# First shift and scale in two halves, small loads on SyncE's queue, branch hints for the first expert and inside overflow blocks

## The chip, the cores and the metric

The kernel runs on one core of a Trainium2 chip. The metric is the device time of one execution in microseconds (us); three executions were timed before the change, and one more was profiled. Engines are named as in the profile: PE is the matrix engine (PEld its weight loads), DVE the vector engine, ACT the scalar engine, POOL the GpSimd engine, SP the engine that issues most transfers. A "q" behind an engine's name means its sequencer (branches, semaphores, issues), not its datapath.

## What is computed

A sequence of 256 tokens with 1024 channels goes through a first block of two layers and a second block of one layer, all in float32. Cut to what matters here:

```python
def first_block(x, c, ...):
    for layer in range(2):
        mod = silu(c) @ w_ada[layer] + b_ada[layer]            # 1024 -> 6 * 1024
        sh1, sc1, g1, sh2, sc2, g2 = split(mod, 6)
        hcur = rms_norm(x, norm1_g) * (1 + sc1) + sh1
        mix = ...   # layer 0: dilated attention and gated MLP; layer 1: convolution and stick-breaking attention
        x = x + g1 * mix
        hcur = rms_norm(x, norm2_g) * (1 + sc2) + sh2
        x = x + g2 * hierarchical_moe(hcur, ...)                # 16 experts, 2 per token, routed by small matrices
    return rms_norm(x, final_norm_g)
# second_block: one layer with eight projections, a recurrence, window attention, and a final norm
```

Every weight is used once, so some 350 MB are streamed from memory in one execution.

## The kernel before

**Streams.** The large weights are cut into tiles of 1 MB (128 x 2048 float32) and loaded by SP through a ring of buffers, in one fixed list (`plan`) that is also the order of their use. `load` (L208) issues the next tile as soon as a buffer is free. All of SP's transfers share one queue, q1, in the order of their issue. POOL's transfers are on another queue, q0. `bcast` (L335) loads a row into all partitions.

**Shift and scale.** `ada` (a generator, matmuls on L351) multiplies the conditioning vector with w_ada: eight tiles of 256 columns give sh1 and sc1 of a layer, 16 records of the profile for each tile (8 matmuls). Behind the eighth, ACT copies the sum (`e`, L364), PE turns it into columns (L369), and `done` (L391 to L393, DVE) makes the vectors b1 and a1 of 8 columns each, one column for 128 channels. In layer 0 this stands at the very start. The rest of w_ada follows as filler work between other matmuls, by a generator (`fill_with`, `some_fill`).

**First projection.** `to_hT` (L536) transposes the scaled x on PE (L553); for each of eight groups k of 128 channels ACT makes `xh` = a1 * x + b1, rounded (L556), DVE the same unrounded (`hf`, L560) and the difference `xl` (L546). The projections (`proj_ws`, L461 to L463, output `pw`; `half_ts`, L478 to L480, output `pt`) multiply xh and xl with weights that ACT and DVE split likewise into `wh` (L444) and `wl` (L447).

**Before the experts.** The last projection of a layer is `out_proj` (`pt` again); its epilogue on DVE is L570 and L571. `moe_consts` loads the router's matrix `wr` (L600) and multiplies it by the shift b2 on PE (`rbias`, L603); `logits` transposes the new x (`tr`, L615) and multiplies it with `wr`.

**Experts.** `moe` runs the 16 experts in order on batches of 64 slots. An expert's hidden half is made by `half` (L806, L807 on PE, L818 on DVE), turned by `turn` (L825 on PE, L826 on DVE), and multiplied down and scattered. Ahead of each expert's second half stands an If (L907, `more`) on the number of its overflow blocks: a block of 64 more slots runs in it, and a further If stands inside that one. Engines read the count from memory (`values_load`, L939 and L968). For experts 1 to 15 a hint that names the coming branch and its direction is given on PE at L969, right behind the load of the count. The first expert's branch and the inner ones have none. Before the first expert's branch DVE and ACT copy x into the accumulators `z` (L949, L951).

The order of instructions on PE, ACT and DVE is set by a list scheduler when the kernel is built, but for stretches under `manual_schedule`, which keep the order of the code.

## Time and profile before

| | |
|---|---|
| median of three runs | 1229.49 us (1227.82, 1229.49, 1229.55) |
| profiled execution | 1227.14 us, of which 1225.4 us span |
| mean granted clock of PE | 0.977 of full speed |
| PE busy | 1118.5 us, 91% |
| DVE, ACT busy | 52%, 34% |
| moved by DMA | 353 MB, 288 GB/s in the mean |

The span is the time from the first to the last instruction of the profiled execution; its own time is 1.7 us longer. [...]

### The profile page before, as it was taken

What the parts mean: (1) busy time and instruction counts of PE and PEld (TensorE: products, weight loads), DVE (VectorE), ACT (ScalarE), POOL (GpSimd) and SP (SyncE); (2) the same over time, 40 slices, a digit from 0 to 9 for tenths busy, and PEclk for the clock granted to TensorE, in tenths of its full rate; (3) what the DMA queues carried; (4) which work ended last, traced back from release to release, by engine and by line L of the source; (5) the groups of instructions that cost most, each with busy time, mean ns of one, the idle gap of its engine ahead of it and who ended that gap; (6) DMA issues with size and microseconds to landing.
All of it is one profiled execution on the core that took longest, in us unless ns stands there. A gap on an engine that the chain in (4) does not pass through costs nothing. (4 is left out here: it accounts for less than half of the span.)

```text
span 1225.4 us, 20762 instructions
## 1 busy us (share of the span) xinstructions
PE 1118.5 (91%) x8164; PEld 798.3 (65%) x8168; DVE 643.1 (52%) x1485; ACT 415.4 (34%) x801; POOL 16.6 (1%) x37
## 2 busy tenths in 40 slices
PE   4899998898999889999987999898889999999996
PEld 2687575454555458867654555554478889887895
DVE  2665463232332258977622333232398787656666
ACT  1433532111111144365311211111356535445553
POOL 1000000000000000000000000000000000000000
PEclk9899998999999999999998999999999989999999
DMA  9999688999999986768855999998455435544340
GB/s 346 419 421 362 248 333 329 405 381 391 399 416 418 383 315 252 264 210 313 345 219 214 404 403 416 390 400 311 163 208 181 143 128 179 182 144 165 127 172 35
DMA packets 50184, 353.38 MB, mean 288 GB/s; under 512 B 5776, under 2 KB 5952, under 8 KB 8416
## 3 DMA queue, kind: packets, MB, share of 16 engines
q1 hardware_dynamic: 47952, 344.14, 72.0%
q0 software_dynamic: 1776, 6.48, 1.7%
q8 instruction: 105, 1.72, 0.6%
q14 instruction: 63, 0.52, 0.1%
q10 hardware_dynamic: 288, 0.52, 0.1%
HBM read 350.07 MB, written 1.05 MB: 287 GB/s over the span
## 5 line engine op out<-in xcount | busy, mean ns | idle before, releaser
L807 PE MATMUL gu<-ring,xg 128*64 128x256 f32 x1024 | 246.2, 395 | 6.3 <-issue 6.3
L806 PE MATMUL gu<-ring,xg 128*64 128x256 f32 x1024 | 246.2, 395 | 1.4 <-issue 1.3
L461 PE MATMUL pw<-xh,wh 128*128 128x256 f32 x736 | 213.1, 291 | 9.6 <-ACT wh L444 4.3
L463 PE MATMUL pw<-xh,wl 128*128 128x256 f32 x736 | 211.4, 288 | 1.7 <-DVE wl L447 1.7
L462 PE MATMUL pw<-xl,wh 128*128 128x256 f32 x736 | 210.6, 287 | 0.0
L447 DVE TENSOR_TENSOR wl<-ring,wh 128x1024 fp32r<-128x1024 f32 x144 | 175.3, 1222 | 66.2 <-ACT wh L444 62.3
L806 PEld LDWEIGHTS gu<-ring,xg 128*64 128x64 f32 x1024 | 141.8, 142 | 73.7 <-issue 16.3
L444 ACT ACTIVATE wh<-ring 128x1024 fp32r<-128x1024 f32 x114 | 120.0, 1058 | 144.4 <-PE pw L462 83.8
L807 PEld LDWEIGHTS gu<-ring,xg 128*64 128x64 f32 x1024 | 142.3, 142 | 22.3 <-issue 12.7
L461 PEld LDWEIGHTS pw<-xh,wh 128*128 128x128 f32 x736 | 142.6, 194 | 21.4 <-issue 11.3
L463 PEld LDWEIGHTS pw<-xh,wl 128*128 128x128 f32 x736 | 143.0, 194 | 6.0 <-DVE wl L447 3.5
L462 PEld LDWEIGHTS pw<-xl,wh 128*128 128x128 f32 x736 | 142.9, 194 | 1.8 <-DVE xl L546 1.0
L832 PE MATMUL y<-ring,ht 128*64 128x512 f32 (+1 forms) x576 | 128.7, 564 | 7.0 <-DVE ht L826 5.0
L818 DVE SCALAR_TENSOR_TENSOR hd<-hs,gc,gu 64x256 f32<-64x256 f32 x64 | 30.7, 479 | 176.5 <-ACT hs L817 176.5
L817 ACT ACTIVATE hs<-gu 64x256 f32<-64x256 f32 x66 | 24.9, 378 | 270.4 <-PE gu L807 270.4
L351 PE MATMUL ada<-ring,zc 128*32 128x256 f32 x960 | 70.8, 400 | 19.8 <-DVE rt L518 13.7
L832 PEld LDWEIGHTS y<-ring,ht 128*64 128x64 f32 x576 | 40.4, 137 | 53.2 <-issue 33.4
L842 ACT ACTIVATE Y<-yf 64x512 fp32r<-64x512 f32 (+1 forms) x72 | 42.7, 593 | 91.3 <-DVE yf L839 90.4
L478 PE MATMUL pt<-wh,xh 128*128 128x512 f32 x144 | 57.9, 403 | 0.6 <-ACT wh L444 0.4
L843 DVE TENSOR_TENSOR Y<-yf,Y 64x512 fp32r<-64x512 f32 (+1 forms) x72 | 46.2, 641 | 22.7 <-ACT Y L842 21.3
L826 DVE COPY ht<-hidT 128x128 f32<-128x128 f32 x66 | 19.2, 292 | 73.2 <-PE hidT L825 73.2
L351 PEld LDWEIGHTS ada<-ring,zc 128*32 128x32 f32 x960 | 27.9, 112 | 45.6 <-DVE sp__111 L326 13.7
(392 smaller groups left out, 1579.8 us busy)
## 6 DMA issues: line engine op xcount, KB each, us to landing
ring<-moe SPq DMA_DIRECT2D x192, 1024.0 KB, 9.1
ring<-ada SPq DMA_DIRECT2D x60, 1024.0 KB, 7.8
ring<-b_z SPq DMA_DIRECT2D x24, 1024.0 KB, 4.8
ring<-b_x SPq DMA_DIRECT2D x12, 1024.0 KB, 4.8
ring<-od_q SPq DMA_DIRECT2D x8, 1024.0 KB, 7.9
ring<-ev_q SPq DMA_DIRECT2D x6, 1024.0 KB, 19.8
ring<-ev_v SPq DMA_DIRECT2D x4, 1024.0 KB, 17.0
ring<-ev_o SPq DMA_DIRECT2D x4, 1024.0 KB, 10.5
```

The source lines that it names most:

```text
L351: T.matmul(p[32 * j:32 * j + 32, :256], zc[:, k, 7 - r:39 - r], w[:, k], start=start and k < 4, stop=stop and k >= 4, skip_group_check=True)
L444: S.activation(h, w, AF.Copy)
L447: V.tensor_tensor(l, w, h.bitcast(F32), op=OP.subtract)
L461: T.matmul(p, hk, xh[:, k], start=k == 0, stop=False)
L462: T.matmul(p, hk, xl[:, k], start=False, stop=False)
L463: T.matmul(p, lk, xh[:, k], start=False, stop=k == KD - 1)
L478: T.matmul(p[t], xh[:, k, n], hk, start=k == 0, stop=False)
L806: T.matmul(p[gs_], xg[:, k], wg[:, k], start=k == 0, stop=k == KD - 1)
L807: T.matmul(p[us], xg[:, k], wu[:, k], start=k == 0, stop=k == KD - 1)
L832: T.matmul(y[64 * h:64 * h + 64, cs], ht[:, k], wd[:, k % 2, h, cs], start=k == 0 and cs.start == 0, stop=k == 3, skip_group_check=cs != s ...
L842: S.activation(Y[a, h, cs], yf[a, cs], AF.Copy)
L843: V.tensor_tensor(Y[b, h, cs], yf[a, cs], Y[a, h, cs].bitcast(F32), op=OP.subtract)
```

## The change

It has three parts. The first one: the eight tiles of layer 0's first shift and scale are loaded in the order 0, 1, 4, 5, 2, 3, 6, 7, and a1 and b1 of layer 0 become two tiles of four columns each, so that the first four tiles give the first half of both. The second: `rbias` (20 KB), `g2dup` (two times 128 KB) and `wr` of both layers (80 KB each) are loaded by SP and no longer by POOL. The third: hints on PE for the first expert's branch and inside overflow blocks.

```diff
@@ -120,7 +120,7 @@
-    A["ada0"] = _ada(i["w_ada"][0])
+    A["ada0"] = _ada(i["w_ada"][0], (0, 1, 4, 5, 2, 3, 6, 7))
@@ -354,22 +354,23 @@
-        if cols:
+        for n, done in cols:
             p = bank(fill["tag"][0], "ada")
-            for t in range(8):
-                ada_rows(p, tile_of(t), t, t == 0, t == 7)
-                if t == 7:
+            for t in range(n):
+                ada_rows(p, tile_of(t), t, t == 0, t == n - 1)
+                if t == n - 1:
                     e = adap.tile([P, 256], F32, name="e", tag="e")
                     S.activation(e, p[:, :256], AF.Copy)
...
             for c in range(2):
-                T.matmul(p[:, 256 + 8 * c:264 + 8 * c], e[:, c * P:c * P + P], sel8, start=True, stop=True, skip_group_check=True)
-            cols(p[:, 256:272].rearrange("p (c t) -> p t c", c=2))
+                T.matmul(p[:, 256 + n * c:256 + n + n * c], e[:, c * P:c * P + P], sel8[:, 0:n], start=True, stop=True, skip_group_check=True)
+            done(p[:, 256:256 + 2 * n].rearrange("p (c t) -> p t c", c=2))
             yield
-            t0 += 8
+            t0 += n
@@ -387,11 +388,18 @@
+        if isinstance(a, tuple):
+            return [part(a[h], b[h], 4 * h) for h in range(2)]
+        return [part(a, b, 0)]
@@ -428,7 +436,9 @@
+    for n in ("a1_0", "b1_0"):
+        mod[n] = tuple(cst.tile([P, 4], F32, name=f"{n}_{h}") for h in range(2))
@@ -553,11 +564,11 @@
-            high = S.activation(xh[:, k], q, AF.Identity, scale=a[:, k:k + 1], bias=b[:, k:k + 1])
+            high = S.activation(xh[:, k], q, AF.Identity, scale=at(a, k), bias=at(b, k))
@@ -588,8 +599,6 @@
-    bcast(rbias.rearrange("p a b -> p (a b)"), A["rows"][0, 0:40])
@@ -597,7 +606,7 @@
-        G.dma_start(wr, A[f"rt{l}"])
+        nc.sync.dma_start(wr, A[f"rt{l}"])
@@ -859,7 +868,9 @@
-            def more_tokens(e, w, b):
+            def more_tokens(e, w, b, nv):
+                if b < 3:
+                    tc.mark_branch_hint_location(f"more{l}_{e}_{b + 1}", hint=nv > b, engines=[mybir.EngineType.PE])
@@ -904,9 +915,9 @@
-                    with tc.If(nv > b - 1, label=None if b > 1 else f"more{l}_{e}"):
+                    with tc.If(nv > b - 1, label=f"more{l}_{e}" + (f"_{b}" if b > 1 else "")):
@@ -937,6 +948,7 @@
             nv = nc.values_load(xi[0:1, 0:1], min_val=0, max_val=3)
+            tc.mark_branch_hint_location(f"more{l}_0", hint=nv > 0, engines=[mybir.EngineType.PE])
@@ -1040,13 +1052,14 @@
+        bcast(rbias.rearrange("p a b -> p (a b)"), A["rows"][0, 0:40], nc.sync)
...
-            bcast(g2dup[64 * h:64 * h + 64], A["drows"][5, h * 512:h * 512 + 512])
+            bcast(g2dup[64 * h:64 * h + 64], A["drows"][5, h * 512:h * 512 + 512], nc.sync)
```

Since the scheduler orders the instructions, the change shows in two places. On ACT, at the first shift and scale, this stood before (`e` is the copy of the projected sum, `wh` the rounded part of the first projection's weights):

```order
L364 ACTIVATE e<-ada 128x256
L556 ACTIVATE xh<-tr,b_0_175,a_0_174 128x256 x5
L444 ACTIVATE wh<-ring 128x1024
L556 ACTIVATE xh<-tr,b_0_175,a_0_174 128x256
L444 ACTIVATE wh<-ring 128x1024
L556 ACTIVATE xh<-tr,b_0_175,a_0_174 128x256 x2
L444 ACTIVATE wh<-ring 128x1024
```

After the change there are two copies `e`, the first four `xh` stand ahead of the second, and two `xh` stand between it and the first `wh`:

```order
L365 ACTIVATE e<-ada 128x256
L567 ACTIVATE xh<-tr,b_0_0_176,a_0_0_174 128x256 x4
L365 ACTIVATE e<-ada 128x256
L567 ACTIVATE xh<-tr,b_0_1_177,a_0_1_175 128x256 x2
L454 ACTIVATE wh<-ring 128x1024
L567 ACTIVATE xh<-tr,b_0_1_177,a_0_1_175 128x256
L454 ACTIVATE wh<-ring 128x1024
L567 ACTIVATE xh<-tr,b_0_1_177,a_0_1_175 128x256
```

Ahead of the first `wh` of ACT there were five `xh` behind the last `e`; there are two now. On PE, at the end of layer 0's attention and the start of its output projection (`ptt` and `po` are the attention's transposes and outputs, `pt` the output projection, `ada` the next layer's shift and scale), this stood before:

```order
L409 MATMUL ada<-e,sel_107 64x256
L603 MATMUL rbias<-wr,b_0_177 128x20 x3
L1154 MATMUL po<-pb,vg 64x256
L1155 MATMUL po<-pb,vg 64x128
L603 MATMUL rbias<-wr,b_0_177 128x20 x5
L1151 MATMUL ptt<-ident,sb 128x128 x3
L478 MATMUL pt_1414<-wh,xh 128x512
L479 MATMUL pt_1414<-wh,xl 128x512
L480 MATMUL pt_1414<-wl,xh 128x512
L1154 MATMUL po<-pb,vg 64x256
L1155 MATMUL po<-pb,vg 64x128
L478 MATMUL pt_1415<-wh,xh 128x512
L1151 MATMUL ptt<-ident,sb 128x128 x3
```

And this stands there after the change:

```order
L417 MATMUL ada<-e,sel_107 64x256
L1167 MATMUL po<-pb,vg 64x256
L1168 MATMUL po<-pb,vg 64x128
L1164 MATMUL ptt<-ident,sb 128x128 x3
L1167 MATMUL po<-pb,vg 64x256
L1168 MATMUL po<-pb,vg 64x128
L1164 MATMUL ptt<-ident,sb 128x128 x3
L1167 MATMUL po<-pb,vg 64x256
L1168 MATMUL po<-pb,vg 64x128
L351 MATMUL ada<-ring,zc 32x256 x16
L612 MATMUL rbias<-wr,b_0_179 128x20 x8
L488 MATMUL pt_1424<-wh,xh 128x512
```

The eight `rbias` matmuls and the first `pt` stood among the attention's last steps. Now they follow the last `po`, behind 16 `ada` matmuls that stood later: one of them among the second half's `pt`, 15 behind the last of these. On SP, `rbias` now follows `rows`, the two `g2dup` stand behind eight further tiles, and `wr` of layer 0 stands between the last `ada` tile and the first of the experts' tiles.

## Rows read from the trace of the kernel before

**Rows 1.** Windows over the front of layer 0, columns in the first row.
```profile
core 0: us, PE busy (x) PEld busy (x) DVE busy (x) ACT busy (x) POOL busy (x), PEclk, DMA share, GB/s
2.00:14.00 12.00, 0.27 (x4) 0.23 (x8) 5.53 (x43) 3.43 (x12) 2.29 (x5) 1.00 0.98 300
14.00:26.00 12.00, 11.62 (x112) 6.85 (x104) 1.91 (x15) 0.00 (x0) 0.00 (x0) 1.00 1.02 421
...
44.00:130.00 86.00, 85.23 (x666) 65.74 (x658) 53.17 (x123) 33.49 (x57) 0.63 (x1) 1.00 0.96 387
```

**Rows 2.** PE's timeline: start, length, engine, line, tiles, records, idle time before and releaser.
```profile
32.05 1.52 PE L351 MATMUL ada<-ring,zc 128*32 128x256 f32 x16 [0.58 <-DMA ring<-ada]
...
38.67 0.58 PE L461 MATMUL pw<-xh,wh 128*128 128x256 f32 x1 [3.97 <-ACT wh L444]
```

**Rows 3.** ACT's timeline of the same stretch.
```profile
35.29 2.38 ACT L556 ACTIVATE xh<-tr,b,a 128x256 fp32r<-128x256 f32 x5 [1.25 <-DVE a L393]
37.55 1.07 ACT L444 ACTIVATE wh<-ring 128x1024 fp32r<-128x1024 f32 x1
```

**Rows 4.** POOL's queue, 0 to 70 us: packets, MB, share of 16 engines.
```profile
q0 software_dynamic: 176, 0.36, 3.4%
```

**Rows 5.** PE's timeline around the router's bias product.
```profile
140.52 1.29 PE L603 MATMUL rbias<-wr,b 128*128 128x20 f32 x10
...
143.16 0.77 PE L478 MATMUL pt<-wh,xh 128*128 128x512 f32 x1
...
147.91 0.38 PE L1155 MATMUL po<-pb,vg 128*64 128x128 f32 x2
```

**Rows 6.** PE's timeline behind the last product of the output projection.
```profile
172.14 1.93 PE L351 MATMUL ada<-ring,zc 128*32 128x256 f32 x30
...
174.56 0.99 PE L615 MATMUL tr<-ident,x 128*128 128x128 f32 x7 [0.24 <-DVE x L571]
```

**Rows 7.** The experts' Ifs (L907), sequencers: count, shortest/median/longest ns, first and last start.
```profile
L907 PEldq COMPARE_BRANCH  x34: 80/444/5846, 194.5 to 868.4; - x34
```

**Rows 8.** The same line, layer 1's first expert alone.
```profile
L907 PEldq COMPARE_BRANCH  x1: 5583/5583/5583, 610.5 to 610.5; - x1
...
L907 DVEq EVENT_SEMAPHORE  x1: 21/21/21, 614.5 to 614.5; - x1
L907 PEldq EVENT_SEMAPHORE  x1: 51/51/51, 616.1 to 616.1; - x1
```

**Rows 9.** PE's timeline: its first work behind five Ifs.
```profile
200.65 0.44 PE L825 MATMUL hidT<-ident,hd 64*128 64x64 f32 x2 [3.71 <-PEq L907]
...
232.70 0.30 PE L825 MATMUL hidT<-ident,hd 64*128 64x64 f32 x2 [2.15 <-PEq L907]
...
283.32 0.31 PE L825 MATMUL hidT<-ident,hd 64*128 64x64 f32 x2 [1.81 <-PEq L907]
...
359.04 0.31 PE L825 MATMUL hidT<-ident,hd 64*128 64x64 f32 x2 [0.47 <-DVEq L907]
...
654.74 0.45 PE L825 MATMUL hidT<-ident,hd 64*128 64x64 f32 x2 [3.57 <-PEq L907]
```

**Rows 10.** Windows behind these Ifs and layer 1's first, columns as in the first.
```profile
200.00:210.00 10.00, 9.11 (x46) 4.61 (x46) 1.25 (x4) 0.38 (x1) 0.00 (x0) 0.66 0.68 234
230.00:240.00 10.00, 7.54 (x45) 4.01 (x45) 1.67 (x4) 0.38 (x1) 0.00 (x0) 0.83 1.00 402
280.00:290.00 10.00, 7.88 (x56) 4.24 (x53) 1.91 (x5) 0.75 (x2) 0.00 (x0) 1.00 0.97 375
610.00:620.00 10.00, 5.93 (x37) 3.33 (x36) 3.61 (x11) 1.58 (x4) 0.00 (x0) 0.84 0.64 243
650.00:660.00 10.00, 6.05 (x28) 3.45 (x30) 1.36 (x4) 0.15 (x1) 0.00 (x0) 0.71 0.49 175
```

**Rows 11.** Issues of 134 to 160 us: line, count, KB each, median us to landing.
```profile
ring<-ada SPq DMA_DIRECT2D x1, 1024.0 KB, 4.8
```

## The prediction

> **What bounds the kernel now.** The page's share of busy time (91% for PE, in the table above) says that PE is the engine to follow, but not where it waits, so I read three kinds of views: the timeline and windows of the start, since all the rest waits for the first shift and scale; PE's timeline where the change moves instructions; and the Ifs of the experts, on the sequencers and on PE's timeline behind them.

> At the start the DMA is the limit. From 2 to 14 us its engines are fully taken (share 0.98), yet they move 300 GB/s, against 421 GB/s from 14 to 26 us at the same share [rows 1]. PE waits for the last projection tile until 32.05 us, and then idles 3.97 us before the first product at 38.67 us, released by ACT's `wh` [rows 2]. ACT makes five `xh` in 2.38 us ahead of that `wh` [rows 3]. From 44 to 130 us PE is busy for 85.23 of 86.00 us [rows 1]: from there it is PE, not a tile, that sets the pace, and a head start at 38 us is carried along.

> In the expert stage the long waits of PE stand behind Ifs. PE's branch instruction takes 444 ns in the median and 5846 ns at most [rows 7]. The unhinted branch of layer 1's first expert takes 5583 ns [rows 8]. PE's first work behind the unhinted ones came after 3.71 us (layer 0's first expert) and 3.57 us (an inner If, behind the only overflow block that ran); a hinted one shows 0.47 us [rows 9].

> **The change part by part. First, the small loads.** At the full rate the bytes of 2 to 14 us would have taken 12 x (421 - 300) / 421 = 3.4 us less [rows 1]. POOL's queue moved only 0.36 MB, but took 3.4% of the engines over 70 us, which is 2.4 us of all of them [rows 4]. If these loads stand behind, the eight tiles land earlier by something between 0.36 MB / 421 GB/s = 0.9 us (the bytes alone) and 3.4 us (the whole deficit). I take 2.9, the middle between the 2.4 us that the queue held the engines and the whole deficit, since other short rows (`cols`, x) run in that time too. In their new places these loads can cost later tiles up to the same 2.4 us. That is hidden as long as PE is the bound, and between 44 and 130 us PE's idle time was 0.8 us in all.

> **The two halves.** Three `xh` fewer stand between the last `e` and the first `wh`. One costs (37.55 - 35.29) / 5 = 0.45 us [rows 3], so `wh` comes 1.4 us sooner; the other `xh` run while tiles 5 to 8 land. The additional `e`, two matmuls and three small DVE operations lie in the same wait. If the wait before the first product then ends on DVE's `hf` or `wl`, this is 0. Together the start gains 4.3 us (bounds 0.9 and 4.8).

> **What the scheduler moved at the output projection.** Before, PE began `pt` at 143.16 us among the attention's last steps, and seven `pt` had run when the last `po` ended at 148.29 us [rows 5]. A `pt` takes (172.14 - 148.29) / 89 = 0.27 us, other matmuls included, so the projection stood as if started at 146.4 us without a hole [rows 5, 6]. Now PE first finishes the attention, then runs 16 `ada` and eight `rbias` matmuls, then `pt`. Sixteen `ada` are 32 records, at 1.93 us for 30 [rows 6] 2.1 us; eight `rbias` are 16 records, at 1.29 us for ten [rows 5] again 2.1 us. The attention's end moves up from 148.3 to 146.4 us, since the seven `pt` are gone from between, so `pt` begins at 146.4 + 4.2 = 150.6 us: a loss of 4.2 us. It is 2.9 if the ten records of `rbias` that stood ahead of the last two transposes had also delayed the chain, and 6.1 if the chain, which waits for DVE, doesn't move up at all. I take 4.2. Before, 30 of these `ada` records filled PE's wait for the new x on DVE, from 172.14 us to the transposes at 174.56 us [rows 6]; that wait stays and is empty now. Behind pauses of this size the clock sometimes fell: after 1.81 us of waiting it was 1.00 over the next window, after 2.15 us it was 0.83, or 1.7 us of 10 lost [rows 9, 10]. I put the mean, 0.85 us, on it (bounds 0 and 1.7). So the front of layer 0 as a whole: 4.3 - 4.2 - 0.85 = -0.75 us, a slight loss.

> **The hints.** With a quick branch, PE still has to wait for DVE, which passes the end of the same If only behind its copies into `z`. In layer 1 DVE is through at 614.5 us and PE at 616.1 us [rows 8]: 1.6 us can be gained, and about 2.0 us of pause stay. Layer 0's pause is 0.1 us longer (3.71 us, [rows 9]; the copies are the same), so 1.7 there. The inner If has no such copies: 3.57 - 0.47 = 3.1 us [rows 9]. Together 6.4 us (bounds 0 and 6.4). The hint instruction itself is one of a sequencer that runs ahead of PE here; I give it nothing. The same wait for DVE is what comes next in both first experts.

> Behind these pauses PE ran at a lower clock: 0.66, 0.84 and 0.71 of full speed in the windows from 200, 610 and 650 us [rows 10], so that up to 3.4 + 1.6 + 2.9 = 7.9 us of the 30 were lost. The inner If's pause goes nearly wholly. The two others shrink to about 2.0 us, after which by the two rows above 0 to 1.7 us are still lost, 1.7 for both in the mean: 6.2 us would come back. I take two thirds, 4.2 us, because part of that low clock stems from PE's other pauses there, as at 200 to 210 us before work picks up (bounds 0 and 7.9).

> **Sum.** -0.75 + 6.4 + 4.2 = 9.85 us. The profiled execution would take 1227.14 - 9.85 = 1217.3 us. It lay 2.35 us under the median of the runs shown, so the median goes to 1229.49 - 9.85 = 1219.6 us. With all terms at their good ends the gain is 4.8 - 2.9 + 6.4 + 7.9 = 16.2 us, or 1213.3 us.

> **Rivals.** (a) *The clock does not come back.* The pauses that stay, about 2 us in the first experts, are as long as those after which the clock was at 0.83 [rows 9, 10]. Against it: 1.81 us left it at 1.00, and the third pause goes. Then 6.4 - 0.75 = 5.65 us are gained: 1223.8 us. Chance 0.20.

> (b) *The inner hint is lost.* Between that hint, at the block's head, and its branch lies a whole expert's work, whereas the hints of experts 1 to 15 stand half an expert ahead. Even of those some branches are slow: 2.15 and 1.81 us of pause behind two hinted Ifs [rows 9]. The 3.1 us and two thirds of 2.9 us of clock then stay: 9.85 - 5.0 gives 4.85 us, 1224.6 us. Chance 0.12. [...]

> (c) *Moving the small loads frees nothing.* The share of the DMA engines was 0.98 already in that stretch; they are the same engines, and the deficit may be that of `cols` and x, which stay. Then only the bytes, 0.9 us instead of 2.9, are gained, and the time is 1221.6 us. Chance 0.12. [...]

> (d) *No hint takes.* Should the long branches come from something else than the missing hint, such as the place of the code, the hints change nothing: 1229.49 + 0.75 = 1230.2 us. That only the unhinted branches in the rows exceed 3.5 us of pause speaks against it. Chance 0.07.

> (e) *Slower, by a hole at the router's bias.* PE runs in order, and behind the first `rbias` matmul stand all 96 `pt`. `wr` was loaded at the very start; now it comes behind the next layer's eight `ada` tiles. If it lands late, the whole projection waits. The change becomes slower by 0.2% only from a landing 12.3 us later than PE's arrival at about 148.5 us, thus from 161 us on; landing at 165 us, 16.5 us late, it gives 1236.1 us. Against it: the last of those tiles, issued behind 134 us, landed after 4.8 us [rows 11], and `wr` is a twelfth of its size. Chance 0.04.

> **How the numbers follow.** The forecast holds 0.45, with a range of its own from 1214 to 1222 us. The rivals (a) to (c) lie between it and 1225 us, two of them together at 1226. The range from 1212 to 1226.5 us takes these in; (d), (e) and part of the pairs are left out. A measurement of this kernel can tell about 0.2%, or 2.5 us, from no change. Faster by more: the forecast, (a), (b), (c) and little else, 0.86; within it (d) and unlucky pairs, 0.09; slower: (e) and (d) with a larger loss at the output projection, 0.05.

> **What would show it.** In the changed profile: the first product near 34.4 us instead of 38.67; the first `pt` behind `rbias` near 150.6 - 4.3 = 146.3 us, and an idle PE of some 2.4 us before the transposes; pauses of about 2 us behind the first experts' Ifs, released by DVE's sequencer, and of 0.5 us behind the inner one; a clock over 0.85 behind all three. The prediction is wrong if the branches stay at 5 us, or if the reshuffled order opens a wait that none of these rows shows.

## The result, and the profile after

The changed kernel takes 1213.20 us in the median of five runs (1206.12 to 1214.40), beside 1229.49 us for the kernel before, also run five times: a ratio of 0.986, with a 95% interval from 0.983 to 0.989. It is 16.3 us faster; 9.85 us were forecast, with a range that holds the result. The profiled execution is the fastest of the five, 1206.12 us with a span of 1204.1 us.

Windows over the changed kernel, with the columns that the first row names:

```profile
core 0: us, PE busy (x) PEld busy (x) DVE busy (x) ACT busy (x) POOL busy (x), PEclk, DMA share, GB/s
2.00:14.00 12.00, 2.87 (x20) 1.62 (x21) 7.43 (x56) 3.44 (x12) 0.06 (x1) 1.00 0.99 392
14.00:26.00 12.00, 11.26 (x130) 6.87 (x128) 1.93 (x7) 1.97 (x4) 0.00 (x0) 1.00 1.01 421
...
175.00:180.00 5.00, 4.78 (x19) 3.65 (x20) 3.20 (x27) 2.26 (x3) 0.00 (x0) 0.50 0.14 46
...
200.00:210.00 10.00, 8.90 (x52) 4.46 (x54) 1.68 (x5) 0.38 (x1) 0.00 (x0) 0.83 0.85 292
601.00:611.00 10.00, 8.80 (x63) 4.50 (x65) 2.49 (x6) 0.38 (x1) 0.00 (x0) 1.00 0.96 354
635.00:645.00 10.00, 8.91 (x64) 4.60 (x66) 2.24 (x5) 0.38 (x1) 0.00 (x0) 1.00 0.86 292
```

From 2 to 14 us the DMA moves 392 GB/s where it moved 300 [rows 1]. Behind the first experts' Ifs and the inner one the granted clock is 0.83, 1.00 and 1.00, where it was 0.66, 0.84 and 0.71 [rows 10]. In the row of 175 us it reads 0.50, and the same in each single microsecond from 175 to 180 us. Before, the same stretch read 1.00; the dip stands where the change emptied a wait, as the timelines below show.

PE's timeline at the start of the changed kernel (start, length, engine, line, tiles, records, idle time and releaser), and ACT's:

```profile
27.92 1.07 PE L351 MATMUL ada<-ring,zc 128*32 128x256 f32 x16 [1.67 <-DMA ring<-ada]
...
32.75 0.58 PE L471 MATMUL pw<-xh,wh 128*128 128x256 f32 x1 [2.59 <-ACT wh L454]
```

```profile
29.11 0.38 ACT L365 ACTIVATE e<-ada 128x256 f32<-128x256 f32 x1 [2.09 <-PE ada L351]
30.73 1.02 ACT L567 ACTIVATE xh<-tr,b,a 128x256 fp32r<-128x256 f32 x2 [1.23 <-DVE a L397]
31.64 1.05 ACT L454 ACTIVATE wh<-ring 128x1024 fp32r<-128x1024 f32 x1
```

The last tile's matmuls start at 27.92 us instead of 32.05 [rows 2], and the first product at 32.75 instead of 38.67 us [rows 2]. Between ACT's last `e` and its first `wh` stand two `xh` where five stood [rows 3].

PE at the output projection of layer 0, and behind its last `pt` (L488 to L490 are the `pt`, L612 the router's bias product):

```profile
140.80 3.00 PE L351 MATMUL ada<-ring,zc 128*32 128x256 f32 x32
143.73 1.96 PE L612 MATMUL rbias<-wr,b 128*128 128x20 f32 x16
145.54 0.48 PE L488 MATMUL pt<-wh,xh 128*128 128x512 f32 x1
...
170.43 0.39 PE L490 MATMUL pt<-wl,xh 128*128 128x512 f32 x1
171.74 0.30 PE L624 MATMUL tr<-ident,x 128*128 128x128 f32 x1 [0.92 <-DVE x L582]
173.17 1.27 PE L624 MATMUL tr<-ident,x 128*128 128x128 f32 x7 [1.13 <-DVE x L582]
```

The output projection's first `pt` starts at 145.54 us, 2.4 us later than before [rows 5], although the kernel's first product came 5.9 us earlier. The last starts at 170.43 us. Behind it PE waits for DVE with nothing in between; the 30 `ada` records of [rows 6] are gone from there. The last transposes are at 173.17 us, 1.4 us before those of [rows 6]. By the end of the router's logits, at the clock of 0.50 shown above, this is gone too: they end at 178.10 us, before at 177.85 us.

PE's first work behind four Ifs of the experts (layer 0's first, an early hinted one, layer 1's first, the inner one):

```profile
200.35 0.31 PE L834 MATMUL hidT<-ident,hd 64*128 64x64 f32 x2 [1.84 <-DVEq L918]
...
229.99 0.30 PE L834 MATMUL hidT<-ident,hd 64*128 64x64 f32 x2 [0.82 <-PEq L918]
...
601.50 0.30 PE L834 MATMUL hidT<-ident,hd 64*128 64x64 f32 x2 [1.84 <-DVEq L918]
...
635.33 0.30 PE L834 MATMUL hidT<-ident,hd 64*128 64x64 f32 x2 [0.55 <-PEq L918]
```

The first experts' Ifs cost 1.84 us each (before 3.71 and 3.62 us), and the releaser is now DVE's sequencer; the inner one costs 0.55 us (3.57 [rows 9]). The hinted one of 2.15 us [rows 9] has shrunk to 0.82 us, which no part of the change was meant to do.

Following PE's `hidT` matmuls through both traces, the 21.5 us between the profiled executions (measured at PE's last matmul, 1215.8 and 1194.2 us) fall into these stretches:

| stretch, by PE | before to after, us |
|---|---|
| to the end of layer 0's logits | +0.3 |
| from there to the second half of layer 0's first expert | -1.7 |
| on to the second half of its last expert | -10.9 |
| on to the end of layer 1's logits | -1.0 |
| layer 1's first expert | -3.1 |
| the If with the overflow block, to the next half | -5.7 |
| all the rest | +0.6 |

The third row, half of it all, was in no term of the forecast. Windows over this stretch of time, before and then after (columns as above):

```profile
212.00:420.00 208.00, 189.45 (x1324) 107.97 (x1320) 63.90 (x129) 34.19 (x66) 0.00 (x0) 0.98 1.00 403
```

```profile
212.00:420.00 208.00, 195.01 (x1390) 109.93 (x1388) 66.88 (x140) 35.60 (x70) 0.00 (x0) 1.00 1.01 413
```

PE is busy for 195.0 instead of 189.5 of 208 us, its clock is 1.00 instead of 0.98, and the DMA moves 413 instead of 403 GB/s, at a share of 1.01. Whether the change as such does this, or something that came with it, is what most of the runs below are about.

### The profile page after: what moved, and what is told of

It reads as the page before. It is cut to its first block, busy times and chain, and to the rows that moved or that the text cites. A ratio compares the mean times of both kernels' runs of the same rounds, so it can differ in the third digit from the quotient of the medians.

```text
span 1204.1 us, 20780 instructions
## 1 busy us (share of the span) xinstructions
PE 1111.1 (92%) x8168; PEld 794.1 (66%) x8172; DVE 644.1 (53%) x1488; ACT 416.2 (35%) x802; POOL 14.1 (1%) x32
## 5 line engine op out<-in xcount | busy, mean ns | idle before, releaser
L816 PE MATMUL gu<-ring,xg 128*64 128x256 f32 x1024 | 237.3, 385 | 2.0 <-issue 2.0
L815 PE MATMUL gu<-ring,xg 128*64 128x256 f32 x1024 | 236.9, 385 | 1.7 <-issue 1.6
L457 DVE TENSOR_TENSOR wl<-ring,wh 128x1024 fp32r<-128x1024 f32 x144 | 175.2, 1222 | 71.9 <-ACT wh L454 68.0
L815 PEld LDWEIGHTS gu<-ring,xg 128*64 128x64 f32 x1024 | 138.1, 138 | 68.6 <-issue 8.4
L816 PEld LDWEIGHTS gu<-ring,xg 128*64 128x64 f32 x1024 | 138.2, 138 | 18.9 <-issue 10.3
L488 PE MATMUL pt<-wh,xh 128*128 128x512 f32 x144 | 57.3, 399 | 0.8 <-ACT wh L454 0.4
L490 PE MATMUL pt<-wl,xh 128*128 128x512 f32 x144 | 56.3, 392 | 0.5 <-DVE wl L457 0.5
L489 PE MATMUL pt<-wh,xl 128*128 128x512 f32 x144 | 56.3, 391 | 0.0
```

The costliest lines, as they stand in the source:

```text
L457: V.tensor_tensor(l, w, h.bitcast(F32), op=OP.subtract)
L488: T.matmul(p[t], xh[:, k, n], hk, start=k == 0, stop=False)
L489: T.matmul(p[t], xl[:, k, n], hk, start=False, stop=False)
L490: T.matmul(p[t], xh[:, k, n], lk, start=False, stop=k == KD - 1)
L815: T.matmul(p[gs_], xg[:, k], wg[:, k], start=k == 0, stop=k == KD - 1)
L816: T.matmul(p[us], xg[:, k], wu[:, k], start=k == 0, stop=k == KD - 1)
```

## The experiments

A number that returns is the time of layer 0's experts, from the second half of the first to that of the last. It is the distance of two rows of PE's timeline; those of the changed kernel:

```profile
208.18 0.33 PE L834 MATMUL hidT<-ident,hd 64*128 64x64 f32 x2
...
428.87 0.34 PE L834 MATMUL hidT<-ident,hd 64*128 64x64 f32 x2
```

That is 428.87 - 208.18 = 220.7 us; before it was 441.20 - 209.62 = 231.6 us. All runs together, with their medians in us. Each ratio is to runs of the kernel before that were timed beside that kernel. The stages are read in the same way from one profile of each kernel, and three kernels were run only once:

| kernel | time | ratio to before (95%) | first product | end of layer 0's logits | experts of layer 0 |
|---|---|---|---|---|---|
| before | 1229.49 | | 38.7 | 177.9 | 231.6 |
| changed | 1213.20 | 0.986 (0.983 to 0.989) | 32.8 | 178.1 | 220.7 |
| e1: changed, again | 1214.59 | 0.988 (0.983 to 0.993) | 32.4 | 178.7 | 220.6 |
| e2: hints only | 1226.42 | 0.999 (0.996 to 1.002) | 39.1 | 179.6 | 236.8 |
| e5: hints only, 4 tiny matmuls | 1213.07 | 0.986 (0.982 to 0.989) | 39.1 | 179.3 | 221.1 |
| e6: changed, 32 tiny matmuls | 1230.54 | 1.001 (0.999 to 1.002) | 33.1 | 178.2 | 237.3 |
| e3: changed, no new hints | 1230.45 | 1.001 (0.999 to 1.003) | 32.6 | 178.9 | 231.6 |
| e4: changed, `wr` on POOL | 1205.89 | 0.980 (0.975 to 0.985) | 32.8 | 172.4 | 220.3 |
| e12: as e4, 32 tiny matmuls | 1227.70 | 0.999 (0.996 to 1.002) | 33.2 | 173.0 | 239.0 |
| e10: before, 4 tiny matmuls | 1228.17 | 1.001 (0.998 to 1.004) | 39.1 | 179.6 | 228.8 |
| e11: before, 32 tiny matmuls | 1228.60 | 1.000 (0.997 to 1.002) | 40.4 | 180.2 | 228.9 |
| e7: before, `wr` on SP | 1236.44 | one run | 39.7 | 185.2 | 230.0 |
| e8: before, two halves | 1221.51 | one run | 38.6 | 175.4 | 231.2 |
| e9: before, `rbias` and `g2dup` on SP | 1233.29 | one run | 35.7 | 175.7 | 237.3 |

**e1, the changed kernel once more**

Nothing is edited. 

> The changed kernel unaltered, profiled once more. Its five runs spread from 1206.1 to 1214.4 us, and the first profile belongs to the fastest. If the short and long branches behind hinted Ifs vary from execution to execution, this profile shows other pauses (over 0.8 us, in the expert stage) than the first one, and the time lies near 1213. If they are set by the code alone, the same pauses return at the same experts, and the 7 us between the runs lie elsewhere. The pauses of 1.84 us behind the two first experts' Ifs return in either case.

The experts of layer 0 again, columns as above:

```profile
212.00:420.00 208.00, 195.10 (x1390) 109.96 (x1388) 67.19 (x140) 35.03 (x69) 0.00 (x0) 1.00 1.01 414
```

Layer 0's experts take 220.6 us again, with the same busy time: what was won there belongs to this program, not to one execution. The pauses of 1.84 us are back. The difference between the two profiled executions lies elsewhere. By the same marks, of the 8.2 us between their ends 0.9 arise up to layer 0's last expert, 1.2 from there to the end of layer 1's logits, 1.8 over layer 1's first expert, 1.3 at the If with the overflow block and 2.9 in layer 1's later experts (217.6 instead of 214.7 us).

**e2, the hints alone**

```diff
--- before
+++ e2
+                if b < 3:
+                    tc.mark_branch_hint_location(f"more{l}_{e}_{b + 1}", hint=nv > b, engines=[mybir.EngineType.PE])
...
-                    with tc.If(nv > b - 1, label=None if b > 1 else f"more{l}_{e}"):
+                    with tc.If(nv > b - 1, label=f"more{l}_{e}" + (f"_{b}" if b > 1 else "")):
...
+            tc.mark_branch_hint_location(f"more{l}_0", hint=nv > 0, engines=[mybir.EngineType.PE])
```

> Only the hints, on the kernel before. My terms (6.4 us of pauses, 4.2 us of clock, both seen in the trace after: 1.8, 1.8 and 3.1 us of pauses and some 5 us of clock) give 1229.5 - 10.5 = 1219 us. If the front brought the larger part, the hints alone give no more than 1223 to 1225. If hints shift other branches too, 1212 to 1214.

It takes 1226.42 us, and its interval holds no change at all. In its trace the inner If's pause is gone, and layer 0's first If takes 1.84 us. But PE pauses in the middle of three experts, each three experts behind the last, where the kernel before has two such pauses in layer 0 (1.40 us at 302.50 and 2.54 us at 408.53), and the hint of layer 1's first expert has next to no effect:

```profile
251.85 0.69 PE L806 MATMUL gu<-ring,xg 128*64 128x256 f32 x1 [2.53 <-issue]
...
301.68 0.38 PE L807 MATMUL gu<-ring,xg 128*64 128x256 f32 x1 [2.54 <-issue]
...
352.41 0.43 PE L807 MATMUL gu<-ring,xg 128*64 128x256 f32 x1 [2.01 <-issue]
...
620.45 0.44 PE L825 MATMUL hidT<-ident,hd 64*128 64x64 f32 x2 [3.49 <-PEq L909]
```

Released by "issue" means that PE waited for nothing that the profile shows. Around the first of them, the queues of the DMA (packets, MB, share of 16 engines):

```profile
q1 hardware_dynamic: 145, 1.06, 100.7%
q8 instruction: 1, 0.02, 2.6%
```

One packet of 16 KB on q8, the queue that the view calls "instruction", lies in this pause, between ring packets that take 100.7% of the engines: it runs from 249.50 to 250.57 us, and PE resumes at 251.85. The two other pauses end 1.22 and 1.49 us behind such a packet. Windows over 212 to 420 us:

```profile
212.00:420.00 208.00, 187.70 (x1310) 107.17 (x1308) 62.78 (x128) 33.79 (x66) 0.00 (x0) 0.98 0.98 395
```

PE is busy 187.7 us there, 7.3 us less than in the changed kernel, with the same hints. So hints alone don't make the stage quick, and all three expectations for this run missed.

**e3, the changed kernel without the new hints**

```diff
--- after
+++ e3
-                if b < 3:
-                    tc.mark_branch_hint_location(f"more{l}_{e}_{b + 1}", hint=nv > b, engines=[mybir.EngineType.PE])
...
-                    with tc.If(nv > b - 1, label=f"more{l}_{e}" + (f"_{b}" if b > 1 else "")):
+                    with tc.If(nv > b - 1, label=None if b > 1 else f"more{l}_{e}"):
...
-            tc.mark_branch_hint_location(f"more{l}_0", hint=nv > 0, engines=[mybir.EngineType.PE])
```

> The changed kernel without any hint: halves and small loads alone. My theory: the start is 5.9 us earlier, but the router's bias product behind the attention and the emptied wait before the transposes take it all back, and 1 to 2 us more through the clock, so 1229 to 1232 us. Rival: the head start is carried, 1223 to 1224 us.

1230.45 us, as the theory said: the first product comes 6.1 us sooner, and the logits end 1.1 us later than before. The front alone brings nothing. But front (+1 us or so) and hints (-2 us) don't add up to -16 us.

**e4, the router's matrix back on POOL's queue**

```diff
--- after
+++ e4
-        nc.sync.dma_start(wr, A[f"rt{l}"])
+        G.dma_start(wr, A[f"rt{l}"])
```

> The changed kernel with the router's matrix on POOL's queue as before; nothing else is undone. The scheduler then puts the bias product among the attention's last steps again. My theory: the 5.8 us lost there and some 1.5 us behind the transposes come back: 1206 to 1208 us. Rival: the order there does not matter, or the load at the start costs the tiles 1 us or more again: 1211 to 1214 us.

1205.89 us, 8.7 us less than e1, which is the changed kernel. PE's timeline at the output projection:

```profile
133.12 0.84 PE L612 MATMUL rbias<-wr,b 128*128 128x20 f32 x6
...
134.69 1.29 PE L612 MATMUL rbias<-wr,b 128*128 128x20 f32 x10
...
137.34 0.76 PE L488 MATMUL pt<-wh,xh 128*128 128x512 f32 x1 [0.19 <-DVE g2dup L418]
...
166.70 1.50 PE L351 MATMUL ada<-ring,zc 128*32 128x256 f32 x24
```

The bias product stands among the attention's last steps again, the first `pt` starts at 137.34 us, and 24 records of `ada` fill the wait behind the last `pt`. The logits end at 172.4 us, 5.4 us earlier than before: all but 0.4 us of the start's 5.9 us arrive there. The load of `wr` at the start costs the first product nothing (32.79 and 32.75 us).

**e5 and e6, the same instructions at another place**

In both, tiny matmuls stand at the very start of PE's program, where PE idles until 10.34 us in the changed kernel and until 13.73 us in the kernel before; nothing uses their result. Apart from them, the order of instructions on all five engines is that of e2 and of the changed kernel.

```diff
--- e2
+++ e5
     V.memset(onesb, 1.0)
+    pad = bank("D", "pad")
+    for _ in range(4):
+        T.matmul(pad[:, 0:1], onesb, onesb[:, 0:1], start=True, stop=True, skip_group_check=True)
```

> Only the hints, and four tiny matmuls more at the very start of PE's program, where PE idles for over 10 us; their result is not used. They cost no time of their own, but the code of all experts lies eight instructions further. If the pauses in the experts (2.5, 2.5 and 2.0 us in the middle of three experts of layer 0, each three experts apart, and the long branches) come from where the code lies against the blocks in which it is fetched, they move, shrink or vanish, and the time is another than that of the hints alone by 3 us or more. Rival: they come from the load on the DMA or from the data; then the same pauses stand at the same experts, and the time is that of the hints alone, 1225 to 1228 us.

1213.07 us: 13 us faster than the hints alone, and as fast as the whole change, by four matmuls that do nothing. The pauses of e2 in the middle of the experts of layer 0 are gone:

```profile
212.00:420.00 208.00, 194.97 (x1386) 109.63 (x1384) 66.62 (x139) 35.19 (x69) 0.00 (x0) 1.00 1.01 413
```

PE is busy 195.0 us of this window, at a clock of 1.00, like the changed kernel.

```diff
--- after
+++ e6
     V.memset(onesb, 1.0)
+    pad = bank("D", "pad")
+    for _ in range(32):
+        T.matmul(pad[:, 0:1], onesb, onesb[:, 0:1], start=True, stop=True, skip_group_check=True)
```

> The changed kernel with 32 such matmuls at the start. If the place of the code decides, some of the 11 us that the changed kernel won between the second and the last expert of layer 0 go: other pauses, 1217 to 1230 us. Rival: they belong to the change itself; then the pauses are those of the changed kernel, and 1212 to 1216 us.

1230.54 us: the whole gain of the change is lost by 32 matmuls that do nothing. The first product (33.1 us) and the end of the logits (178.2 us) are within 0.4 us of the changed kernel's. In layer 0's experts the pauses are back, at other experts and again three apart; below them the window:

```profile
235.12 0.68 PE L819 MATMUL gu<-ring,xg 128*64 128x256 f32 x1 [2.58 <-issue]
...
287.86 0.58 PE L818 MATMUL gu<-ring,xg 128*64 128x256 f32 x1 [2.34 <-issue]
...
337.64 0.43 PE L818 MATMUL gu<-ring,xg 128*64 128x256 f32 x1 [1.23 <-issue]
```

```profile
212.00:420.00 208.00, 189.52 (x1300) 108.08 (x1298) 62.36 (x127) 33.70 (x66) 0.00 (x0) 0.97 0.97 391
```

**e7 to e9, the parts of the front one by one**

The first moves only `wr`, as in the diff of e4 with its signs turned. The second has the two halves (the first five pieces of the diff) and no moved load. The third moves only `rbias` and `g2dup`:

```diff
--- before
+++ e9
-    bcast(rbias.rearrange("p a b -> p (a b)"), A["rows"][0, 0:40])
...
+        bcast(rbias.rearrange("p a b -> p (a b)"), A["rows"][0, 0:40], nc.sync)
...
-            bcast(g2dup[64 * h:64 * h + 64], A["drows"][5, h * 512:h * 512 + 512])
+            bcast(g2dup[64 * h:64 * h + 64], A["drows"][5, h * 512:h * 512 + 512], nc.sync)
```

> The kernel before with nothing changed but the router's matrix, now loaded by SP. The scheduler then puts the bias product behind the attention, as in the changed kernel. My theory: the start as before (first product near 38.7 us), but the last bias of the router 9 to 11 us later than before relative to it and the last logits 6 to 8 us later (177.85 before, 184 to 186 here), 1233 to 1238 us. Rival: the loss belongs to the earlier start, with tiles not there yet; then the logits end within 2 us of before.

> The kernel before with the two halves alone; all small loads on POOL. My terms: the first product 1.4 us earlier, near 37.3 us. If the halves bring more than the three xh, near 36 us; if the small loads brought all of the 5.9 us, 38.7 us.

> The kernel before with the router's bias row and g2dup on SP's queue; the router's matrix stays on POOL, one shift and scale, no new hints. If the small loads bring the earlier tiles, the last projection tile's matmuls start 3 us or more before 32.05 us, and the first product comes at 34 to 36 us. If the place of the router's matrix at the start matters as much, only 1 us of that is there.

PE's timeline in e7, around the bias product; then the last projection tile and the first product in e8, and in e9:

```profile
147.98 2.80 PE L351 MATMUL ada<-ring,zc 128*32 128x256 f32 x32
150.71 1.96 PE L603 MATMUL rbias<-wr,b 128*128 128x20 f32 x16
```

```profile
32.50 1.92 PE L351 MATMUL ada<-ring,zc 128*32 128x256 f32 x16 [1.42 <-DMA ring<-ada]
...
38.57 0.58 PE L471 MATMUL pw<-xh,wh 128*128 128x256 f32 x1 [2.59 <-ACT wh L454]
```

```profile
28.21 1.94 PE L351 MATMUL ada<-ring,zc 128*32 128x256 f32 x16 [1.42 <-DMA ring<-ada]
...
35.65 0.58 PE L461 MATMUL pw<-xh,wh 128*128 128x256 f32 x1 [3.97 <-ACT wh L444]
```

In e7 the 16 `ada` and the bias product follow the attention, as in the changed kernel, with the first product at 39.7 us: the new place comes from the load's queue alone, not from the earlier start. The logits end 7.3 us later than before, and it takes 1236.44 us. In e8 the last tile starts 0.45 us later than before and takes 1.92 instead of 1.52 us [rows 2], so that the earlier `wh` is used up: the first product comes 0.1 us sooner. The gain of its one run comes from behind; the scheduler put its `rbias` matmuls at 136.6 us instead of 139.0, and the logits end 2.5 us sooner. In e9 the last tile starts at 28.21 us, 3.8 us sooner, and the first product 3.0 us sooner. The 1233.29 us of its one run come from the experts of layer 0 again, at 237.3 us.

**e10 to e12, tiny matmuls without the new hints, and on the fastest version**

The edit is that of e5 and e6, four and 32 times on the kernel before, and 32 times on e4.

> The kernel before, with four tiny matmuls at the start of PE's program and nothing else. If a shift of the code is worth as much without the new hints, the time moves by 5 us or more in either direction, with other pauses than at 302 and 408 us of layer 0. If the long pauses need the hints of this change, it stays at 1227 to 1231 us. The two waits of 3.7 and 3.6 us behind the first experts' Ifs and that of 3.6 us behind the inner one stay in either case.

> The same with 32 tiny matmuls. By the theory of the place, a second sample of how far the kernel before moves by its place alone: 1220 to 1235 us, and other pauses than with four. By the rival, 1227 to 1231 us.

> The fastest version so far (the change with the router's matrix on POOL) with 32 tiny matmuls at the start. If its 1206 us rest on the place of the code as the changed kernel's 1213 do, it loses 12 to 20 us, as the changed kernel did: 1218 to 1226 us, still under the changed kernel with the same 32 by 6 to 9 us, the share of the router's matrix. If the place matters less here, 1204 to 1212 us.

e10 and e11 are within 0.1% of the kernel before, so the larger move that the theory of the place allowed for them did not come. The long waits behind the three unhinted Ifs stay, at 3.5 to 4.1 us. The other pauses do change: over 0.7 us, they add up to 6.5 and 7.7 us in layer 0's later experts, at partly other experts, where the kernel before has 8.7 us. Layer 0's experts take 228.8 and 228.9 us, between the good and the bad places of the hinted programs. e12 takes 1227.70 us, 21.8 us more than e4. Its pauses:

```profile
229.31 0.43 PE L818 MATMUL gu<-ring,xg 128*64 128x256 f32 x1 [3.32 <-issue]
...
280.02 0.38 PE L818 MATMUL gu<-ring,xg 128*64 128x256 f32 x1 [2.26 <-issue]
...
313.68 0.45 PE L837 MATMUL hidT<-ident,hd 64*128 64x64 f32 x2 [4.59 <-PEq L921]
```

At this place too, all but 0.6 us of e4's earlier end of the logits is kept (173.0 and 172.4 us); all that is lost, is lost in the experts. The difference to e6, 1230.54 us, is 2.8 us; 6 to 9 were expected.

## Why the prediction was right, and where its sizes were off

**The small loads.** The term was 2.9 us, the last tile came 4.1 us sooner (27.92 instead of 32.05 us), 0.7 us beyond the upper bound. Alone, they gave 3.8 us (e9). The bounds were the error: 0.9 us for the bytes and 3.4 us for the missing rate were taken as two readings of one gain, but they add up, to 4.3 us. The rate over 2 to 14 us rose from 300 to 392 GB/s, which is 12 x 92 / 421 = 2.6 us, and the 0.36 MB that no longer stand ahead are 0.9 us more; the remaining 0.6 us isn't explained. The loads of x gain too: ACT's first work on the second tile of x starts at 7.81 us instead of 10.01. Rival (c) is out.

**The halves.** The term of 1.4 us fits the distance from the last `e` to the first product, 5.0 us before and 3.6 us after. Alone (e8) it brought 0.1 us. There the last tile's matmuls started 0.45 us later and took 0.4 us longer, so e8 doesn't show the term by itself. Together with the small loads the halves made 5.9 us at the first product, against the 4.3 us forecast.

**The output projection.** The place and the cause were right, and e7 shows them alone. The size was forecast as 4.2 + 0.85 us; it was 5.9 + 0.3 = 6.2 us to the end of the logits, of which 4.5 us are lost up to the end of the last `pt` (172.2 us before, 170.8 us after) and the rest behind it. The `ada` behind the attention took 3.00 us instead of 2.1, with a clock of 0.85 over 140 to 150 us, the bias product 1.96 instead of 2.1; and the clock behind the emptied wait lost more than the term for it: the row at 175 us reads 0.50 over 5 us. So the front ended at +0.3 us in the first profile and +0.9 in the second; forecast was +0.75 us. The balance was right although both sides were larger, by 1.6 and 1.2 us; that the two errors cancel is luck. Rival (e), a late `wr`, did not come: the bias product follows the `ada` without a wait.

**The hints.** Pauses of 1.84, 1.84 and 0.55 us behind the three Ifs were forecast as 2.0, 2.0 and 0.5, and the wait for DVE's copies took the place of the branch as described. But only the inner branch became quick (0.36 us); those of the two first experts still took 4.04 and 3.12 us, where they had taken 5.85 and 5.58, and ended before DVE was through. The clock came back to 0.83, 1.00 and 1.00, by the windows 1.7 us lost instead of 7.9; in the second profile the same three windows (from 201, 603 and 639 us) read 0.83 each, 5.1 us lost. Together these three stretches won 1.7 + 3.1 + 5.7 = 10.5 us in the first profile, where 6.4 + 4.2 = 10.6 us were forecast; in the second they won 7.1 us. Rivals (b) and (d) are out for this program. But in e2 the same hint left layer 1's first If at 3.49 us, so (d) is true of one If at one place. Rival (a) was seen there too: behind layer 0's first expert e2 gains no time by the clock.

**What failed.** The step is the sentence "The hint instruction itself is one of a sequencer that runs ahead of PE here; I give it nothing." The execution of the hints takes 37 to 48 ns each on PE's sequencer, and costs nothing that can be seen, but they are 66 instructions and as many register instructions more in PE's program, most in blocks that are never run, and with the start's changes they move the code of all experts. That was worth 10.9 us in layer 0 alone, as much as all forecast terms together. That the result lies inside the range is therefore partly luck: at the place of e6 the same change takes 1230.54 us, outside it. The prediction named a "reshuffled order" as what might make it wrong, but gave it no price, and the rows that could have set one were there: hinted Ifs with 2.15 and 1.81 us of pause [rows 9], which I took as given and which the changed program does not have.

**Shown, and left open.** That the place of PE's program decides is shown: e5 and e2, e6 and the changed kernel, e12 and e4 differ in nothing but tiny matmuls ahead of all work, and by 13, 17 and 22 us. The edit's only other trace is the unused tile `pad`, which e10 and e11 have too.

I forecast by the trace's median, 444 ns over 34 branches, 30 of them hinted [rows 7]: for the inner If that held (0.36 us), for the two first experts' only the pause did.

What stays open is what starts such a packet, and so why one place makes it late and another doesn't; why the kernel before moves by only 0.1% when it is shifted, while the programs with hints move by 13 to 22 us; and what the hints are worth apart from the place. Also open is whether layer 0's 220.3 us are the best that a place can give: in that stage the DMA runs at 413 GB/s, close to the 421 GB/s of the filled window at 14 us.

So of the 16.3 us, the three Ifs hold 7 to 10.5 us by the stages of the two profiles, the front about nothing, and the place the rest; at the place of e6 the same change is worth nothing. With `wr` left on POOL, it is 1205.89 us, the fastest version run, and 23.6 us under the kernel before. Of its 7 to 9 us on the changed kernel, 5.7 are there at the end of layer 0's logits, by the order at the output projection; the rest has the same luck.

## What to carry to other kernels

In a long unrolled program with branches, an edit that adds a few instructions moves all code behind it, and that alone can be worth more than the edit (here 13 to 22 us, where the whole change measured 16.3): before a gain is put down to a change, run it with a handful of idle instructions ahead of it, at two or three places, and look for packets of the "instruction" queues that end just before the pauses (here 1.22 to 1.66 us). A load moved to another queue changes what a list scheduler believes about its landing, and so the order of the engines far from it; read that order before pricing the load. A filler that covers a wait can be worth more than its length: behind the emptied wait the clock read 0.50 for 5 us, where it had read 1.00.

## What the runs showed of the hardware

Four matmuls of one column, in a stretch where PE idles, moved the whole execution by 13 us (1226.42 to 1213.07), and 32 of them by 17 and 22 us the other way. PE's granted clock read 0.50 over a whole window of 5 us, from 175 us, behind a wait whose parts were 0.92 and 1.13 us, and although PE was busy for 4.78 us of these 5. A hint does not by itself make a branch quick: of the branches with the new hints, one took 5.64 us, one 0.36. PE's sequencer at layer 1's first expert, in e2 and in the changed kernel (L942 and L951 are the line of the hint, L909 and L918 the If; the first columns are count, shortest, median and longest time in ns, and the start):

```profile
L942 PEldq ALU_OP  x1: 37/37/37, 611.1 to 611.1; - x1
...
L909 PEldq COMPARE_BRANCH  x1: 5639/5639/5639, 614.5 to 614.5; - x1
```

```profile
L951 PEldq ALU_OP  x1: 37/37/37, 593.8 to 593.8; - x1
...
L918 PEldq COMPARE_BRANCH  x1: 3118/3118/3118, 597.2 to 597.2; - x1
```

In both the hint stands 3.4 us ahead of its branch, and the branch takes 5639 ns in the one and 3118 ns in the other. Most of the difference lies in when one packet starts: the packet of q8 before the branch's end starts 2.9 us behind the branch's start in e2 and 0.6 us behind it in the changed kernel, and in both the branch ends 1.5 to 1.6 us after the packet. In the kernel before, without a hint, it starts 3.2 us behind.
